# Moving the input-gate products of a recurrent layer from VectorE to GpSimd

## The chip, the cores and the metric

The kernel runs on one core of a Trainium2 chip. A core has TensorE (PE in the profile, for matrix products; PEld is its weight load), VectorE (DVE), ScalarE (ACT), GpSimd (POOL) and SyncE (SP), which issues the weight loads. Each engine takes its own instructions in the order in which they were written and waits on semaphores where it needs another engine's result. The metric is the time of one execution on the device, in microseconds. The kernel before takes 1526.24 us (median of three runs, 1525.52 to 1527.98).

## The reference

The model is a small encoder in float32: 256 tokens and 16 meta tokens of width 1024, a layer of attention, a recurrent layer, then two more layers (feed-forward, pooling and gated recurrence, feed-forward). The change lies in the recurrent layer. For each of its 2048 channels and two directions it computes

```
xc = conv_b + sum over 4 taps of shifted(u) * conv_w
r  = sigmoid(xc @ w_a + b_a)            # 16 blocks of 128 x 128
i  = sigmoid(xc @ w_x + b_x)            # input gate
log_a = -8 * r * softplus(-lam);  a = exp(log_a)
b  = sqrt(-expm1(2 * log_a)) * i * xc
h[t] = a[t] * h[t-1] + b[t]             # forward, and reversed for direction 1
y  = (h_forward + h_reverse) * silu(gate);  out = y @ w_out
```

The product `i * xc`, the input gate with the convolved input, is what moves.

## The kernel before, in words

Activations stand with channels on the 128 partitions and time along the columns. A float32 product is made of three float32r matmuls: an operand is split into `hi` and `lo`, and PE sums hi·hi, hi·lo and lo·hi. Weights arrive as 128x2048 tiles (`raw`); for each half, 1024 columns, ACT writes `hi` (a copy) and DVE writes `lo` (raw minus hi). There are four `hi` and four `lo` buffers, so PE can be some three pieces behind the casts and never ahead of them.

The order of every engine's work is fixed when the program is built. `Clock` holds a planned time for each engine, `Engine` adds a cost to it for every instruction written, and helpers written as generators (`conv`, `gate`, `units`, `recur`) are resumed when the planned PE time passes the planned end of what they wrote last. So a change of one instruction's planned engine or cost can change the order of others. The plan charges such a product on GpSimd more than twice what it charges on VectorE. It knows nothing of two engines getting in each other's way.

The recurrent layer works in `NG` = 4 groups of `G` = 4 blocks of 128 channels, in the order of `odd_order`: the input products of group 0 (u0), u1, the output-gate products g0, u2, g1, u3, g2, then the output products w0 to w3, g3, w4 to w7. Group by group:

- `conv` scales a block of PSUM into a `work` tile (DVE), clears the tile's two edges (two GpSimd memsets), and makes `xc`: one ACT instruction, then three of DVE.
- `units` lets PE make the gates of each block (`m<-xc,lw`), ACT applies the sigmoid into `r` and `i_`, then Tanh of `r`. After every second block come the two products of this case: `i_ = i_ * xc`, once for the forward half (2 x 272 = 544 columns) and once for the reverse half (512). Exp and Sqrt on ACT follow.
- `recur` takes two blocks: two wide DVE instructions (1056 columns), four scans, a sum, the gating with `sg`, and the split into `oyh`/`oyl`, which PE needs for the output products.

`r`, `i_`, `th` and `aa` are tiles of one list named `big` (128 x 4 x 528), so the product appears in every view as `big<-big,xc`. All instructions are recorded at line 181, that of the recording helper, so rows are told apart by their tiles.

Of the kernel before, what the change touches and what calls it, by code (L numbers as in the profile page):

```python
# [12 lines left out]
ALU = mybir.AluOpType  # L13
# [5 lines left out]
NM = 16  # L19
S = 256  # L20
T = NM + S
# [98 lines left out]
class Clock:  # L120
# [9 lines left out]
    def range(self, ap):  # L130
        dims = list(ap.ap)
        per = dims[0][0] or 1 << 30
        lo = ap.offset % per
        return ap.tensor.name, lo, lo + 1 + sum((n - 1) * abs(s) for s, n in dims[1:])
# [92 lines left out]
class Builder:  # L227
# [871 lines left out]
    def odd(self):  # L1099
        nc, a = self.nc, self.a  # L1100
        tt, ts, stt, act, mm = self.tt, self.ts, self.stt, self.act, self.mm
# [83 lines left out]
        def load_units(c):  # L1185
            if c < 8:
                lws.append(self.pick("lw", 1, 1e30)[0])
                nc.scalar.dma_start(out=lws[-1], in_=a["lru_w"][c])
                if self.cur is not None:
                    self.keep(lws[-1])  # L1190
# [4 lines left out]
        def units():  # L1195
            yield from self.wait("c8")
            for g in range(NG):
                yield from self.wait("xc", g * G)
                xc = xcs[g]
                self.own(xc)  # L1200
                r, i_ = yield from self.grab("big", 2)
                pending = []
                for q in range(G):
                    b = g * G + q
                    yield from self.wait("xc", b)
                    if q % 2 == 0:
                        lw = lws.pop(0)
                        self.own(lw)
                    for d in range(2):
                        w = T if d == 0 else S  # L1210
                        for gate_, dst, bias in ((0, r, "b_a"), (1, i_, "b_x")):
                            ps = yield from self.grab("m")
                            mm(out=ps[:, :w], lhsT=lw[:, q % 2, 2 * gate_ + d, :], rhs=xc[:, q, src[d]], start=True, stop=True)
                            pending.append((self.clock.mark, ps, w, dst[:, q, part[d]], self.v(bias, 16 * d + b)))
                            if len(pending) > 1:
                                yield from sigmoid(*pending.pop(0))
                    if q % 2:
                        self.drop(lw)
                        load_units(b // 2 + 2)
                yield from sigmoid(*pending.pop(0))  # L1220
                th, aa = yield from self.grab("big", 2)
                for q in range(G):
                    for d in range(2):
                        c = 16 * d + g * G + q
                        act(out=th[:, q, part[d]], in_=r[:, q, part[d]], func=AF.Tanh, scale=c8[:, 0, c:c + 1])
                    yield "act"
                    if q % 2:
                        two = slice(q - 1, q + 1)
                        tt(out=i_[:, two, 0:T], in0=i_[:, two, 0:T], in1=xc[:, two, :], op=ALU.mult)
                        tt(out=i_[:, two, T:], in0=i_[:, two, T:], in1=xc[:, two, NM:], op=ALU.mult)  # L1230
                self.drop(xc)
                for q in range(G):
                    for d in range(2):
                        c = 16 * d + g * G + q
                        act(out=aa[:, q, part[d]], in_=r[:, q, part[d]], func=AF.Exp, scale=c8[:, 1, c:c + 1])
                    yield "act"
                self.drop(r)
                over = []
                for q in (0, 2):
                    act(out=th[:, q:q + 2, :], in_=th[:, q:q + 2, :], func=AF.Sqrt, bias=tiny)  # L1240
                    yield "act"
                    if q == 0:
                        self.keep(i_, th, aa)
                    self.spawn(recur(g, q, i_, aa, th, over))

        def sigmoid(end, ps, w, dst, bias):
            yield from self.until(end)
            act(out=dst, in_=ps[:, :w], func=AF.Sigmoid, bias=bias)
            self.drop(ps)
# [50 lines left out]
        self.spawn(self.norm(1, T, (0, P, 2 * P)))  # L1300
        self.spawn(decay_rates())
        self.spawn(units())
        outs = []

# [706 lines left out]
```

## Time and profile before

| What | Value |
|---|---|
| median of three runs | 1526.24 us |
| the profiled execution's own time | 1526.28 us |
| its span | 1524.5 us |
| PE busy | 1492.8 us (98%) |
| DVE busy | 1116.3 us (73%) |
| ACT busy | 903.1 us (59%) |
| POOL busy | 26.2 us (2%) |

A row of a timeline gives start, duration, engine, operation, output and inputs, shape and count, and in brackets how long the engine had been idle before and who ended it. Neighbouring instructions of one engine overlap a little, so the step from one start to the next, not the duration, is what an instruction takes of a full engine. Of matmuls above all the step counts: their durations overlap by more than half.

### The profile page before, as it was taken

Reading aid. Unit: us, or ns where it says so; the run is one execution under the profiler, and the core shown is the slowest. Engines: PE = TensorE matmul, PEld = TensorE weight load, DVE = VectorE, ACT = ScalarE, POOL = GpSimd, SP = SyncE. Lnnn points to the kernel's source line nnn. Section 1 sums busy time; section 2 is a strip of 40 time slices with the busy share of each in tenths; the row PEclk is TensorE's granted clock in tenths of the full one; section 3 lists DMA queues with packets and bytes.
Section 4 is the critical chain, followed back from the end, with each engine's and each line's share of the span. In section 5 each row is a group of like instructions: output and inputs, shape, how many; then the busy total and the mean of one; then the engine's idle time right before and its main releaser. Section 6 shows DMA issues by size and latency. Waiting matters only on the chain.

```text
span 1524.5 us, 31049 instructions
## 1 busy us (share of the span) xinstructions
PE 1492.8 (98%) x12950; PEld 1458.6 (96%) x12950; DVE 1116.3 (73%) x1882; ACT 903.1 (59%) x1435; POOL 26.2 (2%) x68
## 2 busy tenths in 40 slices
PE   8999999999999999999999999999999998999998
PEld 8988899999999999999999999999999998999998
DVE  6977775689997666669887666666666788877754
ACT  7666654689966654575555554455455754555553
POOL 1000000000000000000000000000000000000000
PEclk9999999999999999999999999999999999999999
DMA  6422224544455555554545655655556444456553
GB/s 239 158 90 84 83 84 141 201 159 168 138 170 190 198 201 172 207 175 146 180 164 186 225 184 177 207 193 197 184 176 227 166 140 138 166 184 223 185 171 123
DMA packets 42492, 259.12 MB, mean 170 GB/s; under 512 B 4840, under 2 KB 6256, under 8 KB 18416
## 3 DMA queue, kind: packets, MB, share of 16 engines
q1 hardware_dynamic: 40624, 251.90, 47.6%
q10 hardware_dynamic: 1728, 5.24, 1.0%
q8 instruction: 101, 1.65, 0.4%
q14 instruction: 39, 0.32, 0.1%
HBM read 256.07 MB, written 1.05 MB: 169 GB/s over the span
## 4 chain that ended last, share of the span: by engine, by line
PE 60%; issue 26%; DVE 8%; ACT 4%; DMA 1%; POOL 1%; SPq 0%; ACTq 0%; DVEq 0%; POOLq 0%
PE acc L181 45%; PE m L181 14%; DVE lo L181 3%; ACT hi L181 2%; DVE big L181 2%; DVE kq L181 1%; ACT w L181 1%; ACT L181 1%; ACT xx L181 1%; DVE xx L181 0%; DVE lf L181 0%; DVE work L181 0%; DMA raw<-in_hin_dram 0%; DMA raw<-in_hi_dram 0%; POOL col L181 0%
## 5 line engine op out<-in xcount | busy, mean ns | idle before, releaser
L181 DVE TENSOR_TENSOR lo<-raw,hi 128x1024 fp32r<-128x1024 f32 (+3 forms) x520 | 582.6, 1129 | 248.0 <-ACT hi L181 243.6
L181 ACT ACTIVATE hi<-raw 128x1024 fp32r<-128x1024 f32 (+3 forms) x520 | 501.5, 980 | 286.7 <-PE acc L181 187.9
L181 PE MATMUL acc<-xh,hi 128*128 128x256 f32 (+1 forms) x2096 | 588.4, 281 | 5.6 <-ACT hi L181 5.6
L181 PE MATMUL acc<-xl,hi 128*128 128x256 f32 (+1 forms) x2096 | 589.0, 281 | 0.0
L181 PE MATMUL acc<-xh,lo 128*128 128x256 f32 (+1 forms) x2096 | 587.4, 280 | 0.0
L181 PEld LDWEIGHTS acc<-xh,hi 128*128 128x128 f32 x2096 | 395.0, 188 | 7.0 <-ACT hi L181 5.6
L181 PEld LDWEIGHTS acc<-xl,hi 128*128 128x128 f32 x2096 | 395.1, 188 | 1.3
L181 PEld LDWEIGHTS acc<-xh,lo 128*128 128x128 f32 x2096 | 394.7, 188 | 1.3 <-DVE lo L181 0.2
L181 PE MATMUL acc<-ph,lo 128*128 128x256 f32 x704 | 194.3, 276 | 0.0
L181 PE MATMUL acc<-ph,hi 128*128 128x256 f32 x704 | 194.3, 276 | 0.0
L181 PE MATMUL acc<-pl,hi 128*128 128x256 f32 x704 | 194.3, 276 | 0.0
L181 PEld LDWEIGHTS acc<-ph,lo 128*128 128x128 f32 x704 | 132.2, 188 | 0.0
L181 PEld LDWEIGHTS acc<-ph,hi 128*128 128x128 f32 x704 | 132.2, 188 | 0.0
L181 PEld LDWEIGHTS acc<-pl,hi 128*128 128x128 f32 x704 | 132.2, 188 | 0.0
L181 PE MATMUL m<-xh,lo 128*128 128x256 f32 (+1 forms) x336 | 95.7, 285 | 0.0
L181 PE MATMUL m<-xl,hi 128*128 128x256 f32 (+1 forms) x336 | 95.5, 284 | 0.0
L181 PE MATMUL m<-xh,hi 128*128 128x256 f32 (+1 forms) x336 | 95.2, 283 | 0.0
L181 DVE TENSOR_TENSOR work<-acc,spread 128x256 f32<-128x256 f32 (+1 forms) x108 | 46.0, 427 | 36.5 <-PE acc L181 32.3
L181 ACT ACTIVATE work<-work 128x256 f32<-128x256 f32 (+2 forms) x92 | 37.4, 408 | 51.7 <-DVE work L181 51.4
L181 PEld LDWEIGHTS m<-xh,hi 128*128 128x128 f32 x336 | 63.7, 190 | 0.2
L181 PEld LDWEIGHTS m<-xh,lo 128*128 128x128 f32 x336 | 63.6, 189 | 0.3
L181 PEld LDWEIGHTS m<-xl,hi 128*128 128x128 f32 x336 | 63.6, 189 | 0.1
(359 smaller groups left out, 2242.2 us busy)
## 6 DMA issues: line engine op xcount, KB each, us to landing
raw<-in_ffn_gu_dram SPq DMA_DIRECT2D x88, 1024.0 KB, 4.9
raw<-in_ffn_dn_dram SPq DMA_DIRECT2D x64, 704.0 KB, 4.1
raw<-in_hin_dram SPq DMA_DIRECT2D x32, 1024.0 KB, 4.9
raw<-in_oin_dram SPq DMA_DIRECT2D x16, 1024.0 KB, 4.9
raw<-in_ein_dram SPq DMA_DIRECT2D x12, 1024.0 KB, 4.8
raw<-in_eout_dram SPq DMA_DIRECT2D x8, 1024.0 KB, 4.9
raw<-in_oout_dram SPq DMA_DIRECT2D x8, 1024.0 KB, 4.9
raw<-in_wph_dram SPq DMA_DIRECT2D x8, 1024.0 KB, 4.9
```

Of the source, the lines that this page charges most:

```text
L181: r = f(*args, **kw)
```

## The change

Both products are issued on GpSimd instead of VectorE. Shapes, operands and place in the program text stay.

```diff
@@ -1226,8 +1226,8 @@
                     yield "act"
                     if q % 2:
                         two = slice(q - 1, q + 1)
-                        tt(out=i_[:, two, 0:T], in0=i_[:, two, 0:T], in1=xc[:, two, :], op=ALU.mult)
-                        tt(out=i_[:, two, T:], in0=i_[:, two, T:], in1=xc[:, two, NM:], op=ALU.mult)
+                        nc.gpsimd.tensor_tensor(out=i_[:, two, 0:T], in0=i_[:, two, 0:T], in1=xc[:, two, :], op=ALU.mult)
+                        nc.gpsimd.tensor_tensor(out=i_[:, two, T:], in0=i_[:, two, T:], in1=xc[:, two, NM:], op=ALU.mult)
                 self.drop(xc)
```

In the built program 16 products leave DVE and 16 come to POOL, and the orders of PE, ACT and DVE change from here to the first feed-forward layer behind; the order of SP, which loads the weights, is the same.

On POOL the products stand between the memsets that clear the edges of `work` tiles for `conv`; here are those of groups 0 (tile big_2727) and 1 (big_2731), in the difference.

```order
+L181 TENSOR_TENSOR big_2727<-big_2727,xc_2715 128x2x272
+L181 TENSOR_TENSOR big_2727<-big_2727,xc_2715 128x2x256
 L181 MEMSET work_83 128x2 x2
+L181 TENSOR_TENSOR big_2727<-big_2727,xc_2715 128x2x272
+L181 TENSOR_TENSOR big_2727<-big_2727,xc_2715 128x2x256
 L181 MEMSET work_89 128x2 x2
 L181 MEMSET work_87 128x2 x2
 L181 MEMSET work_84 128x2 x2
+L181 TENSOR_TENSOR big_2731<-big_2731,xc_2716 128x2x272
+L181 TENSOR_TENSOR big_2731<-big_2731,xc_2716 128x2x256
 L181 MEMSET work_88 128x2 x2
```

Memsets that stood one behind another now have pairs of products ahead of them.

On DVE the place of group 0's products (in the convolutions of group 1) closes up, with everything round it as it was.

```order
 L181 TENSOR_TENSOR work_90<-m_67,spread 128x272
 L181 TENSOR_TENSOR lo_79<-raw_73,hi_74 128x1024
-L181 TENSOR_TENSOR big_2727<-big_2727,xc_2715 128x2x272
-L181 TENSOR_TENSOR big_2727<-big_2727,xc_2715 128x2x256
 L181 TENSOR_TENSOR work_83<-acc_64,spread 128x272
 L181 TENSOR_TENSOR lo_80<-raw_73,hi_75 128x1024
 L181 SCALAR_TENSOR_TENSOR xc_2716<-work_90,vec,xc_2716 128x272 x3
-L181 TENSOR_TENSOR big_2727<-big_2727,xc_2715 128x2x272
-L181 TENSOR_TENSOR big_2727<-big_2727,xc_2715 128x2x256
```

The four products are taken out and nothing takes their place.

On PE the gates of group 2 (`xc_2715` by `lw`) stood in a block of four and one of twelve among the input products of group 3; here is the first block, and where it goes.

```order
-L181 MATMUL m_66<-xc_2715,lw_2724 128x272
-L181 MATMUL m_69<-xc_2715,lw_2724 128x272
-L181 MATMUL m_70<-xc_2715,lw_2724 128x256
-L181 MATMUL m_68<-xc_2715,lw_2724 128x256
...
+L181 MATMUL m_66<-xc_2715,lw_2724 128x272
+L181 MATMUL m_69<-xc_2715,lw_2724 128x272
+L181 MATMUL m_70<-xc_2715,lw_2724 128x256
+L181 MATMUL m_68<-xc_2715,lw_2724 128x256
```

They come 14 places later, and the twelve behind them become three pairs and a block of six with other products between.

## Rows read from the trace of the kernel before

**Rows 1.** The page, busy time of each engine, share of the span, instructions.

```profile
PE 1492.8 (98%) x12950; PEld 1458.6 (96%) x12950; DVE 1116.3 (73%) x1882; ACT 903.1 (59%) x1435; POOL 26.2 (2%) x68
```

**Rows 2.** Busy time by stretch of the span; columns in the first row.

```profile
core 0: us, PE busy (x) PEld busy (x) DVE busy (x) ACT busy (x) POOL busy (x), PEclk, DMA share, GB/s
300.00:315.00 15.00, 15.00 (x107) 14.41 (x106) 9.06 (x17) 11.74 (x25) 0.60 (x6) 1.00 0.58 212
315.00:330.00 15.00, 15.00 (x126) 15.00 (x125) 13.18 (x19) 14.92 (x22) 0.40 (x4) 1.00 0.40 140
330.00:450.00 120.00, 115.56 (x857) 110.38 (x856) 117.64 (x160) 102.49 (x168) 0.00 (x0) 0.99 0.46 159
420.00:435.00 15.00, 13.04 (x105) 12.84 (x104) 14.86 (x17) 12.02 (x13) 0.00 (x0) 0.96 0.41 141
```

**Rows 3.** Waits of PE from 330 to 450 us: total, times, longest.

```profile
PE m L181 <- DVE lo L181: 3.2, 3, 2.0
PE m L181 <- ACT big L181: 0.6, 1, 0.6
```

**Rows 4.** Chain that ended last, in order of time: start, us, what.

```profile
377.05 3.08 DVE big L181 x5
390.25 15.03 PE m L181 x98
407.56 4.89 DVE big L181 x8
```

**Rows 5.** Instructions on the tile big: ns min/median/max, first and last start.

```profile
L181 DVE TENSOR_TENSOR big<-big,xc x16: 683/702/726, 314.9 to 417.7; 128x544 f32<-128x544 f32 x8, 128x512 f32<-128x512 f32 x8
```

**Rows 6.** Timeline of DVE at the first products of group 1.

```profile
348.18 1.32 DVE L181 TENSOR_TENSOR big<-big,xc 128x544 f32<-128x544 f32 x2
349.42 0.68 DVE L181 SCALAR_TENSOR_TENSOR sg<-sg,zg 128x512 f32<-128x512 f32 x1
```

**Rows 7.** Groups of DVE from 330 to 450 us: count, busy, mean ns, idle before.

```profile
L181 DVE TENSOR_TENSOR big<-big,xc 128x544 f32<-128x544 f32 (+1 forms) x12 | 7.9, 704 | 0.0
L181 DVE TENSOR_TENSOR work<-acc,spread 128x272 f32<-128x272 f32 x7 | 3.0, 436 | 0.0
L181 DVE TENSOR_TENSOR zg<-acc,spread 128x512 f32<-128x512 f32 x4 | 2.7, 679 | 0.0
L181 DVE TENSOR_TENSOR zg<-m,spread 128x512 f32<-128x512 f32 x2 | 1.4, 684 | 0.0
```

**Rows 8.** Timeline of DVE and POOL in the attention layer, around two GpSimd copies.

```profile
36.26 0.44 DVE L181 TENSOR_TENSOR kpe<-work,work 128x272 f32<-128x272 f32 x1
36.62 0.50 DVE L181 SCALAR_TENSOR_TENSOR latl<-mq,vec,lath 128x272 fp32r<-128x272 f32 x1
37.04 0.65 DVE L181 TENSOR_TENSOR mq<-mq,work 128x272 f32<-128x272 f32 x1
36.85 0.54 POOL L181 COPY kz<-kpe 64x272 f32<-64x272 f32 x1 [13.75 <-DVE kpe L181]
37.44 0.52 POOL L181 COPY kz<-kpe 64x272 f32<-64x272 f32 x1
```

**Rows 9.** Timeline of two equal GpSimd products, and of DVE beside the second.

```profile
467.07 0.70 POOL L181 TENSOR_TENSOR col<-mx,half 128x2 f32<-128x2 f32 x1 [143.36 <-DVE mx L181]
814.85 1.61 POOL L181 TENSOR_TENSOR col<-mx,half 128x2 f32<-128x2 f32 x1 [75.67 <-DVE mx L181]
814.68 1.22 DVE L181 TENSOR_TENSOR lo<-raw,hi 128x1024 fp32r<-128x1024 f32 x1
```

**Rows 10.** Timeline of PE around 434 us.

```profile
434.18 0.42 PE L181 MATMUL m<-oyh,hi 128*128 128x256 f32 x1
434.39 0.42 PE L181 MATMUL m<-oyl,hi 128*128 128x256 f32 x1
437.38 0.28 PE L181 MATMUL m<-oyh,hi 128*128 128x256 f32 x1
437.50 0.28 PE L181 MATMUL m<-oyl,hi 128*128 128x256 f32 x1
```

## What the change is expected to do

> **What bounds the kernel now.** I read the page's busy times first: PE is busy for 98% of the span, DVE for 73% [rows 1]. So over the whole run only PE's idle time can be won, and a relief of DVE counts only where PE waits for DVE. The products stand between 314.9 and 417.7 us [rows 5], so the second view is the busy time by stretch there. The reader is to see two regimes. From 300 to 330 us DVE has room (9.06 and 13.18 us busy of 15 each). From 330 to 450 us it has none: 117.64 of 120 us, while PE is also at work nearly throughout [rows 2]. Both engines are full, and small holes on PE show who is late. The waits say it: in these 120 us PE waits 3.2 us for `lo`, which DVE writes, and 0.6 us for `big`, which ACT writes [rows 3]. The chain of waits agrees: behind 371 us it runs mostly on DVE (five instructions on `big` at 377.05, the eight scans at 407.56), broken once by 15 us of PE from 390 us [rows 4].
>
> There is one loss that the waits don't count. After the longest wait, 2.0 us [rows 3], matmuls of 256 columns start every 0.21 us; from 437.38 us they start every 0.12 [rows 10]. The granted clock of that slice is 0.96 [rows 2]: for a few microseconds PE ran at the lower of its two levels (1.2 GHz) after it had stood idle. From 434.18 to 437.38 us are 3.2 us, that is 15 steps of 0.21, which would have been 1.8 us at 0.12: 1.4 us lost.
>
> **Part 1: what DVE gives up.** Sixteen products leave DVE [rows 5]. Two of them followed by a third instruction take 349.42 - 348.18 = 1.24 us [rows 6], so one takes 0.62 us of a full engine (the 0.70 us of its duration overlaps its neighbours). That is 9.9 us in all. Twelve of them, groups 1 to 3, stand in the full stretch [rows 7]: 12 x 0.62 = 7.4 us. The four of group 0 stand where DVE has 1.8 us of idle time in 15, and are worth nothing to PE.
>
> **Part 2: what GpSimd takes back.** The trace of before has no wide two-input product on GpSimd, but it shows what happens when GpSimd reads SBUF beside DVE. In the attention layer a DVE instruction ends at 36.62 + 0.50 = 37.12 us. A GpSimd copy of 272 columns that began at 36.85 ends at 37.39, 0.27 us later. The DVE product behind it takes 0.65 us where one of the same shape takes 0.44 [rows 8]: 0.21 us longer. The second copy ends 0.27 us after that product (37.04 + 0.65 = 37.69; 37.44 + 0.52 = 37.96). So they take turns: the copy gets 0.27 us between two DVE instructions, and DVE pays for it, less some 0.06 us. The other direction shows in the tiny products of `norm`: 0.70 us with DVE idle, 1.61 us where DVE casts `lo` from 814.68 to 815.90 [rows 9].
>
> A product has 544 or 512 columns and two inputs. I price it as four copies of 272 columns: 4 x 0.27 = 1.08 us, less 0.06 = 1.02 us of delay to DVE; for 512 columns 0.96; 0.99 on average. The low end is one pass for both inputs, 2 x 0.27 - 0.06 = 0.48 us. The high end takes not the 0.27 us but the distance of the two copies' starts, 37.44 - 36.85 = 0.59 us [rows 8]: 4 x 0.59 - 0.06 = 2.30 us. I take 0.99, because the 0.27 us are seen twice and are what DVE was kept waiting for. Not all of DVE's work is kept waiting: instructions that read one input from PSUM (`work`, `zg`) should run beside GpSimd; they are 3.0 + 2.7 + 1.4 = 7.1 us of the 109.7 that stay (117.64 less 7.9) [rows 2, 7], 6%. So the twelve cost 12 x 0.99 x 0.94 = 11.2 us, and DVE ends the full stretch 11.2 - 7.4 = 3.8 us later than it did. It has 2.4 us of idle time there, in pieces under 0.3 us, which I don't count as cover. The four of group 0 cost 4 x (0.93 - 0.62) = 1.2 us, which the idle time before 330 us hides; without that cover they add these 1.2 us.
>
> The Trainium skill prices the product itself: in its GPSIMD Engine Reference (section "3.1 Elementwise — side-by-side cycle accounting") a two-input add of 2048 float32 columns takes 4497 ns on GpSimd against 2293 on VectorE, and elementwise arithmetic is advised against there. No run here shows that; by it, as an estimate, 544 columns would take 1.19 us and 512 1.12, DVE's delay would be 12 x 1.10 x 0.94 = 12.4 us, and the time 1531.4 us.
>
> **Part 3: what the new order moves.** On POOL, memsets that clear edges of `work` now stand behind pairs of products. ACT's first step of `conv` reads these edges, and casts of `hi` are queued behind it on ACT. A pair may end later than planned by the cast of `lo` that it has to let pass (1.22 us [rows 9]); four memsets stand right behind a pair, so up to 4.9 us on ACT. ACT has 17.5 us of idle time from 330 to 450 us [rows 2]: I take 0 and keep the 4.9 for the range. The products themselves are not on a path: `recur` reads them only after eight Exp and a Sqrt on ACT. On PE the gates of group 2 come in smaller portions and later, so their sigmoids should no longer make PE wait: the 0.6 us for `big` go [rows 3]. The low end there is no gain. SP's order is the same, so no DMA moves in its queue.
>
> **The sum.** DVE 3.8 us later, and PE, which waits for its `lo`, with it: +3.8. The gates: -0.6. A longer wait of PE may bring a second stretch at the lower clock (1.4 us); I take half, +0.7. Together +3.9 on the profiled execution's 1526.28 us, which is 0.04 above the median: 1530.2 us, and by itself between 1527.5 and 1534.
>
> **The rivals.**
>
> *GpSimd gets in without cost to DVE.* For it: the DVE instruction that ran when the first copy began was no longer than usual (0.50 us), and DVE's gaps are many. Against it: the 0.65 and the 1.61 us [rows 8, 9]. DVE would be 7.4 us ahead, more than PE can take: it wins its 3.8 us of waits and the 1.4 us of lower clock [rows 3, 10]. 1526.3 - 5.2 = 1521.1 us.
>
> *Price and saving cancel.* If both inputs pass at once, the twelve cost 12 x 0.48 x 0.94 = 5.4 us against 7.4. DVE is 2.0 us ahead, which shortens the wait before 434 us but not the lower clock behind it. About 1524.5 us; any price of 0.55 to 0.8 us lands within the noise. For it: a product's columns are only twice the copy's. Against it: GpSimd would have to read two inputs as fast as one.
>
> *GpSimd holds DVE for much longer*. The distance of the copies' starts, 0.59 us, may be what an instruction really takes [rows 8]. Then a product delays DVE by 2.30 us, and twelve by 12 x 2.30 x 0.94 = 25.9 us: DVE ends 18.5 us later, PE waits for every `lo`, and with one more stretch at the lower clock the time is 1546 us. It turns to a loss from a delay of 0.66 us (0.62 / 0.94). The Trainium skill speaks for this reading: Perfetto Trace Analysis, section "GPSIMD Engine Instruction", calls GpSimd's reported spans unreliable and tells one to time by start-to-start spacing. Against it: between these two starts DVE's product held the second copy up, so the spacing has a wait in it.
>
> **How the numbers follow.** Chances: the forecast 0.53, no cost 0.14, cancel 0.22, much longer 0.11. A measurement of this kernel can tell about 0.2%, 3 us, from no change: below 1523.2 is faster, above 1529.3 slower. Of the forecast's 0.53 some 0.06 fall below 1529.3. Slower: 0.47 + 0.11 = 0.58; same: 0.06 + 0.21 = 0.27; faster: 0.14 + 0.01 = 0.15. The range from 1522.5 to 1539 leaves out about 0.1 on each side: the better part of the first rival, and nearly all of the last.
>
> **What would show it.** Part 1: no `big<-big,xc` on DVE, sixteen on POOL. Part 2: DVE instructions beside a product are longer by about 1 us (a scan of 0.7 us reads 1.7), the mean of the two-input groups rises while `work` and `zg` keep 0.44 and 0.68; the busy time of DVE from 330 to 450 us stays near full though 7.9 us have left. If those means stay, the first rival holds. Part 3: waits of ACT for POOL's memsets under 2 us in all, no wait of PE for `big`. The sum: PE's waits for `lo` in this layer at about 7 us instead of 3.2, and no difference behind the first feed-forward layer. I am wrong if PE's waits shrink, if a product on POOL blocks DVE for under 0.6 us, or if the layer ends later because of ACT.

## The result, and the profile after

The changed kernel takes 1542.51 us (median of four runs, 1542.04 to 1545.7) against 1527.11 for the kernel before (four runs, 1525.52 to 1528.87): a ratio of 1.0104 with a 95% interval of 1.0091 to 1.0117, that is 15.9 us more (0.0104 x 1527.11). The forecast was 3.9 us more, in a range that ended at 1539. The sign was right; the size was not.

The profiled execution took 1542.04 us, 15.8 us more than the one before, with a span of 1540.3. The page's busy times, beside [rows 1]:

```profile
PE 1495.5 (97%) x12950; PEld 1462.1 (95%) x12950; DVE 1119.6 (73%) x1866; ACT 904.0 (59%) x1435; POOL 51.1 (3%) x84
```

Sixteen instructions have left DVE, and its busy time is 3.3 us higher all the same. From 330 to 450 us, as in [rows 2], and the two stretches that follow:

```profile
330.00:450.00 120.00, 113.04 (x834) 108.67 (x832) 113.59 (x135) 99.45 (x164) 20.89 (x22) 0.97 0.43 150
450.00:465.00 15.00, 4.97 (x21) 4.68 (x22) 11.15 (x15) 4.38 (x6) 0.00 (x0) 0.60 0.39 140
465.00:480.00 15.00, 15.00 (x127) 15.00 (x126) 11.95 (x24) 10.01 (x20) 0.00 (x0) 0.94 0.30 98
```

The second row is where the time went: from 450 to 465 us PE works 4.97 of 15 us. PE's waits from 330 to 465 us (total, times, longest), beside [rows 3]:

```profile
PE m L181 <- ACT oyh L181: 10.5, 1, 10.5
PE acc L181 <- DVE work L181: 2.9, 1, 2.9
PE acc L181 <- DVE lo L181: 1.9, 1, 1.9
PE m L181 <- DVE oyl L181: 1.1, 1, 1.1
PE m L181 <- DVE lo L181: 0.5, 1, 0.5
```

For these 135 us the kernel before adds two rows to [rows 3]:

```profile
PE m L181 <- ACT oyh L181: 0.4, 1, 0.4
PE m L181 <- DVE oyl L181: 0.3, 1, 0.3
```

PE's waits went from 4.5 to 16.9 us, and 10.5 of them are a single wait, for `oyh`: that of the first output product that needs the last group's `y`. The waits for `lo`, which the forecast expected to grow to about 7 us, shrank from 3.2 to 2.4.

The two executions can be laid beside each other at that wait. PE up to its end, in the kernel before and then in the changed one (length, busy time with matmuls, granted clock, DMA):

```profile
0.00:447.03 447.03, 433.74 (x3066) 0.99 0.41 141
```

```profile
0.00:458.92 458.92, 434.07 (x3066) 0.98 0.40 140
```

The same 3066 matmuls, 11.9 us later. What follows at the wait in the changed kernel, as a timeline of PE:

```profile
458.93 0.58 PE L181 MATMUL m<-oyh,hi 128*128 128x256 f32 x1 [10.55 <-ACT oyh L181]
460.61 0.58 PE L181 MATMUL m<-oyl,hi 128*128 128x256 f32 x1 [1.10 <-DVE oyl L181]
460.98 0.42 PE L181 MATMUL m<-oyh,lo 128*128 128x256 f32 x1
461.20 0.41 PE L181 MATMUL m<-oyh,hi 128*128 128x256 f32 x1
...
466.74 0.28 PE L181 MATMUL m<-oyh,lo 128*128 128x256 f32 x1
```

The busy times and the granted clock of this stretch:

```profile
460.98:466.74 5.76, 5.76 (x29) 5.76 (x28) 0.93 (x3) 0.36 (x1) 0.00 (x0) 0.50 0.03 13
```

From 460.98 to 466.74 us a step takes 0.21 us, from there on 0.12: PE has stood idle and works at a granted clock of 0.50, the lower of its two levels (1.2 GHz), as at 434 us in the kernel before [rows 10]. (The forecast read 0.96 there from the slice of 420 to 435 us, which holds less than 1 us of that stretch; from 434.18 to 437.38 us the trace has 0.50.) The 5.76 us hold 27 steps, 3.1 us at 0.115: 2.7 us lost. With 11.9 us up to the wait and 0.8 us more for `oyl`, 15.4 of the 15.8 us stand. Behind this layer the waits are nearly as they were (the largest, for `kq`, 7.5 us instead of 6.6).

Why the wait is there shows in the gates. The matmuls of the gates, before and then after (ns min/median/max, first and last start):

```profile
L181 PE MATMUL m<-xc,lw x128: 377/391/497, 296.0 to 406.1; 128*128 128x272 f32 x64, 128*128 128x256 f32 x64
```

```profile
L181 PE MATMUL m<-xc,lw x128: 377/390/437, 295.3 to 417.2; 128*128 128x272 f32 x64, 128*128 128x256 f32 x64
```

And what PE does between the last of them and the wait's end, before and then after:

```profile
406.15:447.03 40.88, 38.29 (x312) 0.96 0.47 157
```

```profile
417.25:458.92 41.67, 31.13 (x266) 0.93 0.45 156
```

From the last gate to a `y` that PE can use it takes about 41 us in both: sigmoid, Tanh, Exp, Sqrt, scans and casts, through ACT and DVE. PE meanwhile runs the output products of earlier groups. In the kernel before it has 312 matmuls for this and arrives 0.4 us too soon; in the changed kernel 46 of them have gone ahead of the last gate (46 x 0.115 = 5.3 us), and it runs dry. The last gate itself comes 11.1 us later: 5.3 us of that are these 46 matmuls, and most of the rest is that PE had already waited 5.3 us ahead of it (the rows for `work` and `lo` above), against 1.6 us in the kernel before. The chain that ended last agrees; its pieces there alternate between DVE and ACT, where in the kernel before the chain between these two points, from 405 to 447 us, runs on DVE but for the last cast:

```profile
417.75 4.74 DVE big L181 x5
...
432.18 1.25 ACT big L181 x4
...
451.66 3.08 DVE big L181 x5
...
460.61 9.48 PE m L181 x56
```

Last, the turns of GpSimd. The products on POOL, for [rows 5]; the shortest 1.29 us, the longest 2.14:

```profile
L181 POOL TENSOR_TENSOR big<-big,xc x16: 1285/1568/2144, 299.6 to 419.2; 128x544 f32<-128x544 f32 x8, 128x512 f32<-128x512 f32 x8
```

DVE's groups from 330 to 450 us (count, busy, mean ns, idle before), for [rows 7]. Before:

```profile
L181 DVE SCALAR_TENSOR_TENSOR xc<-work,vec,xc 128x272 f32<-128x272 f32 x24 | 11.9, 500 | 1.1
L181 DVE TENSOR_TENSOR_SCAN big<-big,big 128x272 f32<-128x272 f32 x16 | 11.3, 708 | 0.0
L181 DVE TENSOR_TENSOR_SCAN big<-big,big 128x256 f32<-128x256 f32 x16 | 10.7, 667 | 0.0
L181 DVE TENSOR_TENSOR big<-big,big 128x1056 f32<-128x1056 f32 x8 | 10.1, 1258 | 0.3
```

After:

```profile
L181 DVE TENSOR_TENSOR_SCAN big<-big,big 128x272 f32<-128x272 f32 x14 | 14.3, 1025 | 0.0
L181 DVE SCALAR_TENSOR_TENSOR xc<-work,vec,xc 128x272 f32<-128x272 f32 x24 | 13.9, 580 | 1.1
L181 DVE TENSOR_TENSOR_SCAN big<-big,big 128x256 f32<-128x256 f32 x14 | 13.6, 973 | 0.0
L181 DVE TENSOR_TENSOR big<-big,big 128x1056 f32<-128x1056 f32 x8 | 12.0, 1498 | 0.7
L181 DVE TENSOR_TENSOR zg<-acc,spread 128x512 f32<-128x512 f32 x4 | 2.7, 683 | 0.0
```

The lengthening sums to 14 x (0.317 + 0.306) + 24 x 0.080 + 8 x 0.240 = 12.6 us, 1.05 us for each of the twelve products of groups 1 to 3. `zg`, which reads PSUM, is as long as before, and so is `work` (429 ns; 436 before).

### The profile page after: what moved, and what is told of

The parts are those of the page before. It is cut to its first block, busy times and chain, and to the rows that moved or that the text cites. A ratio compares the mean times of both kernels' runs of the same rounds, so it can differ in the third digit from the quotient of the medians.

```text
span 1540.3 us, 31056 instructions
## 1 busy us (share of the span) xinstructions
PE 1495.5 (97%) x12950; PEld 1462.1 (95%) x12950; DVE 1119.6 (73%) x1866; ACT 904.0 (59%) x1435; POOL 51.1 (3%) x84
## 3 DMA queue, kind: packets, MB, share of 16 engines
HBM read 256.07 MB, written 1.05 MB: 167 GB/s over the span
## 4 chain that ended last, share of the span: by engine, by line
PE 64%; issue 19%; DVE 9%; ACT 5%; DMA 1%; POOL 0%; POOLq 0%; ACTq 0%; SPq 0%; DVEq 0%
PE acc L181 51%; PE m L181 12%; DVE big L181 3%; DVE lo L181 3%; ACT hi L181 2%; ACT L181 1%; ACT big L181 1%; DVE xc L181 1%; DMA raw<-in_hin_dram 1%; DVE kq L181 1%; ACT w L181 1%; ACT xx L181 0%; DVE xx L181 0%; DVE lf L181 0%; DVE work L181 0%
## 5 line engine op out<-in xcount | busy, mean ns | idle before, releaser
L181 PE MATMUL m<-xh,lo 128*128 128x256 f32 (+1 forms) x352 | 100.0, 284 | 0.0
L181 PE MATMUL m<-xh,hi 128*128 128x256 f32 (+1 forms) x352 | 99.7, 283 | 0.0
L181 PE MATMUL m<-xl,hi 128*128 128x256 f32 (+1 forms) x352 | 99.5, 283 | 0.0
```

Of the source, the lines that this page charges most:

```text
L181: r = f(*args, **kw)
```

## The experiments

Each was timed against the kernel before in three rounds. In `Engine(clock, name, real)` the name says which engine the plan charges, and `real` takes the instruction; so the plan's order and the engine that works can be set apart. Where a diff sets `moved`, both products are written as `nc.moved.tensor_tensor(...)` in place of `tt(...)`.

**The order alone.** The order of the changed kernel on PE and ACT, with the products on VectorE.

```diff
+        self.moved = Engine(clock, "pool", nc.vector)
```

> Order of the changed kernel on PE, ACT and DVE, but the sixteen products are issued on VectorE, so GpSimd does nothing new. If the turn-taking of GpSimd and VectorE makes the 16 us (theory 1), the order alone costs little: 1524 to 1530 us, and PE waits at the end of the recurrent layer for about 1 us. If the new order makes most of it (theory 2: gates of group 2 later on PE, the split of group 2 ahead of group 3's Tanh on ACT), it stays slow: 1535 us or more, with a wait of PE for oyh of several us.

1535.6 us, ratio 1.0041 [1.0027, 1.0055]: 6.3 us lost with nothing on GpSimd. PE's longest wait, and PE from the last gate to that wait's end:

```profile
PE m L181 <- ACT oyh L181: 6.8, 1, 6.8
```

```profile
414.85:452.58 37.73, 30.89 (x266) 0.96 0.43 151
```

The same wait at the same place behind the same 266 matmuls: the order alone makes 6.8 of its 10.5 us.

**GpSimd alone.** The order of the kernel before on PE and ACT, with the products on GpSimd.

```diff
+        self.moved = Engine(clock, "dve", nc.gpsimd)
```

> Order of the kernel before on PE, ACT and DVE (the plan still charges VectorE for the products), but they are issued on GpSimd. Theory 1 (turn-taking): as slow as the changed kernel, 1538 to 1545 us, with about 12 us added to VectorE instructions beside the products. Theory 2 (order): what the prediction priced, about 1530 us.

1534.44 us, 1.0038 [1.0025, 1.0051]: +5.8 us, between what the two theories expected. Its waits:

```profile
PE m L181 <- DVE lo L181: 4.2, 3, 2.4
PE acc L181 <- DVE work L181: 3.7, 2, 2.9
...
PE m L181 <- ACT oyh L181: 0.4, 1, 0.4
```

PE waits for what DVE writes, and for `oyh` no longer than before. Beside the twelve products DVE's instructions are 12.0 us longer in all (1.00 each); less the 7.4 us that left, 4.6.

**The relief alone.** The order of before; the products are written nowhere.

```diff
+class NoOp:
+    def __getattr__(self, op):
+        return lambda *args, **kw: None
...
+        self.moved = Engine(clock, "dve", NoOp())
```

> The sixteen products are left out altogether (the result is not the reference's); order of the kernel before. It shows what relief of VectorE by 9.9 us is worth when nothing takes it back. Both theories: 1520 to 1523 us, PE's waits for lo in the recurrent layer nearly gone. If it stays at 1526, VectorE never set the time there and the prediction's part 1 is wrong.

1526.72 us, 0.9991 [0.9981, 1.0]: nothing that can be told from no change. Both theories missed. DVE's waits from 330 to 450 us say why:

```profile
DVE lo L181 <- ACT hi L181: 6.6, 6, 2.8
```

In the kernel before this row has 0.7 us. DVE, relieved, stands and waits for ACT, which makes `hi` in a fixed order behind its Exp and Tanh.

**The order, with harmless instructions on GpSimd.** The order of the changed kernel; GpSimd fills the same columns with a constant.

```diff
+class Clears:
+    def __init__(self, real):
+        self.real = real
+    def tensor_tensor(self, out, in0, in1, op):
+        return self.real.memset(out, 0.5)
...
+        self.moved = Engine(clock, "pool", Clears(nc.gpsimd))
```

> Order of the changed kernel; in place of each product GpSimd fills the same columns with a constant (the result is not the reference's): it waits and signals as the product does but reads nothing. Theory 1: VectorE is relieved and not held up, 1520 to 1525 us. Theory 2: the order still costs, 1532 us or more. VectorE instructions beside the fills should keep their usual durations.

1531.65 us, 1.0027 [1.0015, 1.0039]: +4.1 us. One place, DVE and POOL. The changed kernel first:

```profile
334.65 2.22 DVE L181 TENSOR_TENSOR big<-big,big 128x1056 f32<-128x1056 f32 x1
336.80 4.69 DVE L181 TENSOR_TENSOR_SCAN big<-big,big 128x272 f32<-128x272 f32 x4
334.19 3.82 POOL L181 TENSOR_TENSOR big<-big,xc 128x544 f32<-128x544 f32 x2 [22.19 <-ACT big L181]
```

And with fills:

```profile
335.99 1.26 DVE L181 TENSOR_TENSOR big<-big,big 128x1056 f32<-128x1056 f32 x1
337.17 2.50 DVE L181 TENSOR_TENSOR_SCAN big<-big,big 128x272 f32<-128x272 f32 x4
337.35 0.53 POOL L217 MEMSET big<- 128x512 f32 x1 [1.30 <-ACT big L181]
```

Beside products that read SBUF four scans take 4.69 us, with a fill among them 2.50. A fill is shorter than a product, so it has less time to get in the way; but with all sixteen fills no group of DVE's instructions is longer than in the kernel before. So it is GpSimd's reading that holds DVE, not its writing or its waiting and signalling. PE still waits 7.4 us for `oyh`: the order still costs, a little less than the 1532 us expected. With the two runs above this is a table of two by two. Without the products on either engine the order costs 0.0036 (1.0027 - 0.9991), 5.5 us; with them on GpSimd 0.0066 (1.0104 - 1.0038), 10.1 us. The difference of the two, 4.6 us, is little more than the intervals allow (some 0.0024, 3.7 us).

**A plan that knows the price.** The products on GpSimd; the plan charges VectorE 1.0 us for each.

```diff
+            if self.name == "pool" and op == "tensor_tensor" and n > 500:
+                at = self.clock.at
+                at["dve"] = max(at["dve"], at["pe"]) + 1.0
...
+        self.moved = Engine(clock, "pool", nc.gpsimd)
```

> Products on GpSimd as in the changed kernel, but the plan also charges VectorE 1.0 us for each, about what the traces show that it loses. The order then comes out with 314 matmuls of PE between the last gate of group 3 and the first output product that needs group 3's result, against 264 in the changed kernel and 310 before. Theory 3 (the new order costs because the gates of group 3 come later and PE has less work to cover their chain; the turn-taking adds its delay): about 1533 us, like the old order with products on GpSimd. If the order's cost lay in something else than this distance: nearer to 1540.

1539.93 us, 1.0086 [1.007, 1.0102]: a miss, so giving back the distance is not enough. 314 matmuls now stand between the last gate and the first that needs its `y`, the wait for `oyh` is gone, and others have come:

```profile
PE m L181 <- DVE lo L181: 5.6, 3, 2.7
PE m L181 <- ACT big L181: 3.5, 2, 2.7
```

The gates of group 2 come so early that PE waits 2.7 us for ACT's sigmoids, which still read the tiles that it is to write, and the casts to `lo` fall behind. Its profiled execution of 1538.13 us also lies 3.5 us above its span of 1534.6, where those of the other runs lie 1.7 to 2.0 above; why stays open.

**Group 0 alone on GpSimd.** The order of before.

```diff
+        self.moved = Engine(clock, "dve", nc.gpsimd)
...
-                        tt(out=i_[:, two, 0:T], ...
+                        (nc.moved.tensor_tensor if g == 0 else tt)(out=i_[:, two, 0:T], ...
```

> Old order on PE and ACT; only the four products of group 0 go to GpSimd, where VectorE has idle time. If a product on GpSimd costs only where VectorE and ScalarE are full: 1525 to 1528 us, no change. If the turn-taking costs wherever it falls: a quarter of 5.8 us, 1528 to 1530.

1527.38 us, 1.0003 [0.9993, 1.0013]: no change. Where DVE has idle time, the four products neither cost nor bring anything that can be told from nothing (2.0 us at most).

**Sixteen more products.** Those of the kernel stay on DVE; GpSimd makes sixteen of the same size from `xc` into a spare tile.

```diff
+        spare = self.t(od, [P, 2, T], "spare", mybir.dt.bfloat16)
...
+                        self.tc.nc.gpsimd.tensor_tensor(out=spare, in0=xc[:, two, :], in1=xc[:, two, :], op=ALU.mult)
+                        self.tc.nc.gpsimd.tensor_tensor(out=spare[:, :, 0:S], in0=xc[:, two, NM:], in1=xc[:, two, NM:], op=ALU.mult)
```

> Old order, products stay on VectorE; GpSimd makes sixteen extra products of the same widths from xc into a spare bfloat16 tile that nobody reads. VectorE loses the turns and gets no relief. If its delay goes to the end one for one: twelve times about 1.05 us, 12 us, 1538 to 1542 us. If relief is worth nothing because ScalarE binds, and delay counts only beyond ScalarE's lead: 1533 to 1536 us, like products moved in the old order.

1535.8 us, 1.0061 [1.0046, 1.0076]: +9.3, between what was expected, and so it decides little. The expectation's twelve were eight: these products wait for `xc` alone, so half of them run before 330 us, and the eight behind lengthen DVE's instructions by 5.8 us, 0.7 each. Why less than 1.05 isn't shown; their output is bfloat16, and both inputs are the same tile. The run does show GpSimd's reading as a loss by itself, with DVE's own work unchanged; PE's waits are for DVE's `lo` (7.2 us).

**Late gates alone.** Nothing on GpSimd; the gates of group 3 wait for 5 us of planned PE time.

```diff
+                if g == NG - 1:
+                    yield from self.until(self.clock.at["pe"] + 5.0)
```

> Products on VectorE and the plan of the kernel before, but the gates of group 3 may only start 5 us of planned PE time later: 259 matmuls are left between the last gate and the first product that needs group 3's result (264 in the changed kernel, 310 before). Nothing goes to GpSimd. Theory 3: 51 matmuls less of cover at 0.115 us, so about 6 us slower, 1531 to 1535 us, with PE waiting for oyh at the end of the layer. If the distance is not the cause of the order's cost: 1526 to 1528 us.

1537.56 us, 1.0072 [1.0053, 1.009]: +11, more than expected. PE's longest wait, and PE from the last gate to that wait's end:

```profile
PE m L181 <- ACT oyh L181: 6.9, 1, 6.9
```

```profile
416.45:453.70 37.25, 30.37 (x261) 0.97 0.49 173
```

The changed kernel's wait, made by the place of the last gates alone. The 11 us stand against 6.3 for the order alone, but in the two traces the layer ends equally late (9.0 and 9.2 us, in the table under "The sum" below): what differs lies behind the layer or in the scatter of executions.

**ACT relieved alone, and both.** First ACT's eight Sqrt go, then these and the products (by the edit of the relief alone).

```diff
+        self.left_out = Engine(clock, "act", NoOp())
...
-                    act(out=th[:, q:q + 2, :], in_=th[:, q:q + 2, :], func=AF.Sqrt, bias=tiny)
+                    nc.left_out.activation(out=th[:, q:q + 2, :], in_=th[:, q:q + 2, :], func=AF.Sqrt, bias=tiny)
```

> Old order; the eight Sqrt of the recurrent layer on ScalarE are left out, 8 x 1.17 us and four table loads of 1.28 us, 14.5 us of ScalarE (the result is not the reference's). VectorE keeps all its work, products too. If VectorE and ScalarE bind together, so that relief of one alone is worth nothing: 1524 to 1527 us. If ScalarE alone binds: 1520 to 1522.

1527.16 us, 0.9994 [0.9985, 1.0004]: nothing that can be told from no change. Part of ACT's new room went into waits for weights, which a DMA brings (7.3 us from 330 to 450, 3.9 before), and for DVE.

> Old order; the eight Sqrt on ScalarE and the sixteen products on VectorE are left out (the result is not the reference's). If the two engines bind together, this gains what neither gains alone: 1519 to 1522 us, close to all that PE loses in this layer (its waits and the lower clock). If PE's waits come from something else, such as weight loads: 1524 to 1527.

1522.84 us, 0.9968 [0.9955, 0.9982]: 4.9 us won, about what was expected. Neither relief alone can be told from no change; both together can. By the times alone it isn't clear that the two win more than their sum (1.4 + 0.9 against 4.9 us, each to within some 1.5 to 2 us); the traces say so, where behind the layer the three runs are 0.2, 1.6 and 4.9 us ahead of the kernel before. DVE and ACT bind this stretch at the same time. In the kernel before there is a piece where neither has room, nor has PE:

```profile
406.00:425.00 19.00, 19.00 (x165) 18.95 (x165) 18.93 (x26) 18.94 (x31) 0.00 (x0) 1.00 0.48 165
```

**Early gates.** Nothing on GpSimd; the plan charges VectorE 0.4 us too much for each product (`more`, a new argument of `Engine`).

```diff
-            self.clock.op(self.name, cost, outs, ins, late)
+            self.clock.op(self.name, cost + self.more, outs, ins, late)
...
+        self.moved = Engine(clock, "dve", nc.vector, 0.4)
```

> Products on VectorE, but the plan charges 0.4 us too much for each; so the gates of groups 2 and 3 come earlier on PE, and 333 matmuls are left between the last gate and the first product that needs group 3's result (310 before). Theory 3 alone: 23 more matmuls of cover, 1523 to 1526 us. If gates that come too early make PE wait for the sigmoids instead: 1528 to 1532 us, with waits of PE for big.

1532.98 us, 1.003 [1.0019, 1.0041]: +4.6, 1 us above the range of the second expectation, with its waits for `big`. 333 matmuls behind the last gate, no wait for `oyh`, but

```profile
PE m L181 <- DVE lo L181: 3.7, 2, 2.3
PE acc L181 <- DVE lo L181: 3.1, 2, 2.5
PE m L181 <- ACT big L181: 1.9, 4, 0.6
```

Both directions lose: the order of before stands between two losses. No version that does all of the kernel's work beat the kernel before.

## Why the prediction was wrong, point by point

**Part 3 is the step that failed.** It priced the new order on PE at -0.6 us, as the wait for `big` that goes. That wait went. But the prediction looked only at the order's first difference, the gates of group 2, and not at where the last gates of group 3 end up: with 46 fewer matmuls behind them. The order alone costs 6.3 us (the first experiment; 9.2 us in its trace, by the end of the layer). The order moves because the plan takes VectorE to be freer: a program, built and not run, that charges GpSimd's products at VectorE's price has the changed kernel's order, row for row. On ACT the cost of 0 was right: it never waits for POOL in this layer. Of the three signs of being wrong that the prediction names, the last came in part: the layer ends later, at a chain through ACT and DVE.

**Part 2, GpSimd's turns, was right.** 0.99 us for each product was forecast, 0.93 after the share that reads PSUM; the trace has 1.05, and 1.00 in the order of before. The rival that priced 2.30 us, and with it the reading of GpSimd by the distance of starts, is refuted, and so are the rivals of no cost and of equal cost. That the 1546 us of the first of these lie nearer to the measured 1542.5 than the forecast does is chance: PE did not wait for every `lo`. Net of the relief the prediction had DVE 3.8 us late; with the order held, the chip says 5.8.

**Part 1, the relief.** 7.4 us were counted for DVE. As a credit against GpSimd's delay they fit (12.0 - 7.4 = 4.6, measured 5.8). As a gain by themselves, on which the first two rivals rest, they are worth nothing that could be measured, because ACT is as full as DVE in parts of that stretch (the relief alone; ACT relieved alone, and both). The prediction read ACT's 17.5 us of idle time in 120 [rows 2] as room; it is an average over stretches of which some have none.

**The sum.** 6.3 for the order and 5.8 for GpSimd make 12.1 us; the measured 15.9 is 3.8 more. The intervals of the three ratios together are about 0.0023 wide to either side, 3.5 us, so this is barely resolved, and other readings leave less. By the plain medians of all executions the two are 8.3 and 7.1 us, and their 15.4 is the changed kernel's 15.4. In the traces one can take the start of the same matmul behind the layer, that after the first 3600:

| Run | Start, us | Later than before, us |
|---|---|---|
| kernel before | 508.39 | |
| the order alone | 517.61 | 9.2 |
| late gates alone | 517.41 | 9.0 |
| GpSimd alone | 513.30 | 4.9 |
| changed kernel | 524.06 | 15.7 |

Here 14.1 of 15.7 us stand. So an interplay of the two is between nothing and some 4 us, and it isn't shown. If there is one, the traces point to a place. From the last gate to the wait's end the chain takes 37.7 us in the new order with the products on VectorE (in an execution of 1538.35 us, the longest of its five), and 41.7 with them on GpSimd. And in the changed kernel ACT meets

```profile
426.08 0.63 ACT L181 ACTIVATE oyh<-big 128x512 fp32r<-128x512 f32 x1 [3.68 <-DVE big L181]
```

a cast of group 2's `y` that waits 3.7 us for a late DVE, with the rest of group 3's gate work on ACT queued behind it; in the order alone the same cast starts at 419.90 us without a wait. Where there is no cover, such lateness can go straight into the end. No run separates this from scatter.

**The lower clock** was priced at 0.7 us, half of one stretch. At the layer's end alone it is 2.7 us, behind an idle time of 10.5 us and not of 2.

## What to carry to other kernels

When an order is planned from costs, a change of engine is two changes: price the new order too, and look at its last dependent stage, by counting the work between the last producer and its first consumer against the length of the chain between them. A relief of one full engine can be worth nothing where a second one is as full; leave out work on each, and on both, before the relief is counted. Work moved to an engine that holds up the first one can cost more than it frees: here 1.05 us for every 0.62 us moved.

## What the runs showed of the hardware

- A GpSimd product of 512 or 544 columns with two inputs takes 1.29 to 1.36 us where little holds it up (group 0 alone on GpSimd), but delays DVE by 1.05 us, less than its duration. Beside DVE it takes up to 2.14 us. The Trainium skill (SBUF — State Buffer, section "Who interferes with whom") says that a VectorE instruction with two SBUF inputs contends with a GpSimd one that reads SBUF and not with one that only writes it, that a VectorE instruction with at most one SBUF input does not contend, and that the ports they share are an exclusive lock. The fills (four scans take 2.50 us, beside products 4.69) and the unchanged `work` and `zg` agree; for the lock the trace has 1.05 us of a product's 1.3.
- A GpSimd fill of 544 columns takes 0.55 us and leaves DVE's scans at 661 to 719 ns (664 to 721 in the kernel before).
- The step of 256-column matmuls stayed at 0.21 us for 5.8 us after PE had stood idle for 10.5 (granted clock 0.50 in these 5.8 us); after the wait of 2.0 us in the kernel before it lasted 3.2 us (0.50 as well).
